# The first two column groups of the per-layer gate as a pair: seven products for eight in three of eight units, with the weights' sums made by VectorE

## The chip, the cores and the metric

The kernel runs on one core of a Trainium2 chip. The metric is the device time of one launch in microseconds (us); the median of three runs counts. PE is TensorE, DVE VectorE, ACT ScalarE, POOL GpSimd and SP SyncE, which here issues DMAs.

## The reference

One layer of a decoder trunk with 256 tokens, width 2048, all in f32. Only the end of it is touched:

```
h = RMSNorm(x);  u = h @ W_in          # ten parts; two of them the merge gates ga, gb
...                                    # two branches: yA (short conv), yB (linear recurrence)
m = sigmoid(gA) * (yA @ WA) + sigmoid(gB) * (yB @ WB);  x = x + m @ W_o
gate = sigmoid(RMSNorm(x) @ W_pg)      # W_pg 2048 x 2048: "the last gate"
x = x + gate * (p @ W_pp);  out = RMSNorm(x)
```

## The kernel before

**Products.** Each f32 operand is cut into two parts of 32-bit type fp32r: hi, a rounded copy (ACT), and lo, what is left (DVE subtracts). A product is a `triple` of matmuls: hi·hi, hi·lo, lo·hi, each 128 x 128 of the activations (loaded as PE's weights) against 512 columns of the weight matrix, summed in a PSUM bank. `put` cuts activations, 256 columns at a time; `cut`, called from `split`, cuts weights.

**Items.** The work is one flat list of items. An item is a chunk `c` of 256 rows of a weight matrix and a column group of 512 columns (`whi`, `wlo`, 128 x 1024: the two halves of 128 rows beside each other); with two halves of tokens that makes four products or 12 matmuls. The groups come in order: PP, the ten parts of W_in, A, B, then O (W_o, four groups of eight items, the first two interlaced) and PG (the last gate, four groups of eight items). The last PG group is not in the loop, but in a tail that orders its halves for the end. In what follows, G is the first item of the last gate (`gate` in the code), G−1 the last item of O's group 3, and so on; O3 is that group, and O2 the one before it, whose last item is G−9.

**The order.** In the loop over `pos`, an item first causes the `split` of the items up to `pos + LEAD` (3 ahead; from `gate` on growing to 8, function `ahead`). Then its matmuls are traced, then loads of raw weights (`load`, SP; three buffers of 1 MB), then `advance()` makes one step of every running epilogue. Epilogues are generators; each `yield` ends a step. A first step is traced at the group's last item, behind that item's `advance()`. A split needs a free pair (whi, wlo): a ring of four in `wp`, and from G+4 on six more in the pool `late`, so that the pair of an item is that of the item four before.

What is traced is put in order by the framework's scheduler, which can move an instruction past others of its engine. `step` makes an epilogue's ACT and DVE work follow the newest split. `pinned(mark)`, called at the end of an item, goes further: it ties each instruction that ACT and DVE got in this item to the one traced before it on that engine, so that traced order is kept; its first tie is to the last instruction of the item before. Before the change this is done from the first pair of merge gates to the end of the last B group, not in O and PG.

**An O epilogue** (`ep_o`, five steps). Step one: DVE adds the two banks to x (L840), ACT squares for the norm (L841) and copies in spread order (L847), SP writes 4 x 128 KB to DRAM (`turn`, L317). Step two: SP issues the reload of 512 KB (L328). Two steps only wait. Step five: a DVE transpose (L321) and four `put`s (L286 ACT, L287 DVE), which make four of the sixteen 128-row pieces of `x1T`, the activations of the last gate. O2's fifth step is traced at G−5, and O3's at G+3.

**A PG epilogue** (`ep_pg`): ACT sigmoid from PSUM, DVE times `pw` and added to x, ACT squares, a step later POOL times the final gain.

**Merge gates as pairs.** Two column groups of W_in (ga, gb) are worked on together for j = 1 to 3: five of the eight chunks are units "S" of Winograd's form, with seven products in place of eight, the others are "C" items with four products for each of the two groups. The seven sums go to eight banks, four of tag `g` and four of tag `s`; `ep_products` and `ep_gates` add them up. A unit needs sums of the tokens' quarters (s1 to s4) and of the weights' quarters (t1 to t4). For these pairs DMAs on POOL's queue add part of the weights (`add_by_dma`), and `combine_weights` does the rest.

Of the kernel before, what the change touches and what calls it, by code (L numbers as in the profile page):

```python
# [15 lines left out]
P = 128  # L16
# [15 lines left out]
SEVEN = [()] + 3 * [(0, 2, 3, 5, 6)]  # L32
TOGETHER = [(0, 1), (1, 2), (3, 2)]
NARROW, Q = len(LEVELS), 32

# [12 lines left out]
def hybrid_kernel(ctx, tc, xT, x, pT, prm, gfin, masks, w_in, w_a, w_b, w_o, w_pg, w_pp, out):  # L48
# [58 lines left out]
    for gi, (kind, j, w, g, op) in enumerate(groups):  # L107
        if kind == "gb" and SEVEN[j]:
            continue
        for c in range(w.shape[2]):  # L110
            it = {"gi": gi, "kind": kind, "j": j, "c": c, "last": c == w.shape[2] - 1}
            if kind != "ga" or not SEVEN[j]:
                key = ("PP", j // 2) if kind == "PP" else (gi, c // 2)
                items.append(dict(it, w=(w, g, c), raw=key, slot=(j if kind == "PP" else c) % 2))
            elif c in SEVEN[j]:
                items.append(dict(it, kind="S", w=(w, g, c), raw=(gi, c)))
# [10 lines left out]
    def raw_of(pos):  # L127
        it = items[pos]
        if it["raw"] not in loaded:
            if it["kind"] == "S":  # L130
                t = tuple(
                    pools["st"].tile([P, n, CW], F32, tag=tag, bufs=bufs, name=nm(tag))
                    for tag, n, bufs in (("sA", 2, 2), ("sB", 1, 3))
                )
            else:
                t = wp.tile([P, 2, 2 * CW], F32, tag="raw", bufs=3, name=nm("raw"))
            loaded[it["raw"]] = t
        return loaded[it["raw"]]

    def load(pos):  # L140
        it = items[pos]
        if it["raw"] not in loaded:
            raw, (w, g, c) = raw_of(pos), it["w"]
            if it["kind"] == "S":
                for n, to in enumerate(raw):
                    nc.sync.dma_start(out=to.rearrange("p n x -> p (n x)"), in_=w[g + n, :, c, n * CW :])
            elif it["kind"] == "C":
                for n in range(2):
                    nc.sync.dma_start(out=raw[:, n, :], in_=w[g + n, :, c, :])
            elif pos < APART:  # L150
                for i in range(2):
                    w, g, c = items[pos + i]["w"]
                    nc.sync.dma_start(out=raw[:, i, :], in_=w[g, :, c, :])
            else:
                nc.sync.dma_start(out=raw, in_=w[g, :, c : c + 2, :])

    def add_by_dma(behind=None):
        pos = next((n for n, it in enumerate(items) if it["kind"] == "S" and n not in pair_sums), None)
        if pos is not None:
# [18 lines left out]
    def pair_of(pool, n, tags=("whi", "wlo"), width=2 * CW):  # L178
        return tuple(pool.tile([P, width], F32R, tag=tag, bufs=n, name=nm(tag)) for tag in tags)

    def cut(hi, lo, src):
        a = nc.scalar.activation(out=hi, in_=src, func=AF.Copy)  # L182
        v = nc.vector.tensor_tensor(out=lo, in0=src, in1=hi.bitcast(F32), op=ALU.subtract)  # L183
        state["splits"] = (a.ins, v.ins)

    def split(pos, halves=(0, 1)):
        it = items[pos]
        load(pos)
        src = raw_of(pos)
        src = src[0].rearrange("p n x -> p (n x)") if it["kind"] == "S" else src[:, it["slot"], :]  # L190
# [21 lines left out]
    last_group = len(items) - w_pg.shape[2]  # L212
    gate = len(items) - 4 * w_pg.shape[2]
    parked = next(n for n, it in enumerate(items) if it["kind"] == "A" and it["j"] == 3)
# [500 lines left out]

    def quarters(j):
        return [state[n][:, t * CW : (t + 1) * CW] for n in ("ga", "gb") for t in range(NT)]

    def ep_products(j, bk):
        for n in ("ga", "gb"):  # L720
            state[n] = t4(n, 1)
        a0, a1, b0, b1 = quarters(j)
# [6 lines left out]
    def ep_gates(j, n, bk):  # L729
        q = quarters(j)  # L730
        for t in range(NT):
            add(q[2 * n + t], q[2 * n + t], bk["c", n, t])
        for t in range(NT):
            d = q[2 * n + t]
            nc.scalar.activation(out=d, in_=d, func=AF.Sigmoid, scale=state["rstd1"][:, t : t + 1])
# [9 lines left out]
    def ep_gb(j, psum):  # L745
        return ep_gate(j, "gb", psum)

    def token_sums():
# [5 lines left out]
        for first, n in TOGETHER:  # L754
# [12 lines left out]
            a11, a12, a21, a22 = Fv[:, :, 0, 0], Fv[:, :, 1, 0], Fv[:, :, 0, 1], Fv[:, :, 1, 1]  # L767
            s1, s2, s3, s4 = (Sv[:, :, i] for i in range(4))
            for out, u, v, op in (
                (s1, a21, a22, ALU.subtract), (s2, s1, a11, ALU.subtract),  # L770
                (s3, a11, a21, ALU.subtract), (s4, a12, s2, ALU.add),
            ):
                nc.vector.tensor_tensor(out=out, in0=u, in1=v, op=op)
            sums_of = tuple(v[:, first : first + n] for v in state["S"])
            fourth = tuple(v[:, 2 * c : 2 * (c + n) : 2, P:] for v in state["hT"])
            for (hi, lo), src in ((sums_of, Sv[:, :, :3]), (fourth, Sv[:, :, 3])):
                nc.scalar.activation(out=hi, in_=src, func=AF.Copy)
                nc.vector.tensor_tensor(out=lo, in0=src, in1=hi.bitcast(F32), op=ALU.subtract)
# [56 lines left out]
    def ep_o(j, psum):  # L835
# [15 lines left out]
        for c in range(4):  # L851
            put(state["x1T"], j * 4 + c, x1[:, c * T : (c + 1) * T], gain(PRM_GPLE, j * 4 + c))
        if j == 3:
            tot = sc(2, "tot2", 1)
# [3 lines left out]
            )  # L858
            state["rstd2"] = rsqrt_of(tot, NT, D, "r2")

    def ep_pp(j, psum):
# [191 lines left out]
    def ahead(pos):  # L1053

        return LEAD + min(max(pos - gate, 0) // 4, 5)

# [10 lines left out]

    def count_products(j):
        order = [it for it in items if it["kind"] in ("S", "C") and it["j"] == j]
        used.clear()  # L1070
# [15 lines left out]
    def unit_products(pos):  # L1086
        it = items[pos]
        c, h = it["c"], state["hT"]

# [10 lines left out]
        b22, t1, t3, t2, t4_ = sums.pop(pos)  # L1100
        s1, s2, s3 = (tuple(v[:, SEVEN[1].index(c), i] for v in state["S"]) for i in range(3))
        s4 = x_of(0, 1)
        for name, op, part in zip(names, (s4, x_of(0, 0), x_of(1, 0), s1, s3, s2, x_of(1, 1)),
# [20 lines left out]
    for pos, it in enumerate(items[:last_group]):  # L1124
        mark = len(nc.cur_bb.bb.instructions)
        kind, j, c, last = (it[n] for n in ("kind", "j", "c", "last"))
        _, _, w, g, opname = groups[it["gi"]]
        nch = w.shape[2]
        if pos == gate:
            close_pool("back")  # L1130
            close_pool("m")
            open_pool("late", "left")
        if pos == parked:
# [4 lines left out]
            active.append(unpark())  # L1138
        if pos + 2 < len(items) and items[pos + 2]["kind"] == "S":
# [22 lines left out]
        if pos >= gate and c == 0:  # L1162
            load_pw(j)
        if pos == FIRST + 4:
# [13 lines left out]
        if kind in ("S", "C"):  # L1178
            if c == 0 and it.get("n", 0) == 0:
                count_products(j)  # L1180
                for name, tag in zip(("P6", ("c", 0, 1), "P5", "P7", "P1", ("c", 0, 0), ("c", 1, 0), ("c", 1, 1)), "ggggssss"):
                    banks[name] = bank(tag)
            if kind == "C" and c == nch - 1 and it["n"] == 0:
                ep_products(j, banks)
            unit_products(pos)
            if kind == "C" and c == nch - 1:
                ep_gates(j, it["n"], banks)
        else:
# [9 lines left out]

        for q in range(done, min(done + AHEAD, len(items)) if pos >= FIRST else 0):
            load(q)  # L1200
# [17 lines left out]
        if last and kind not in ("S", "C"):  # L1218
# [110 lines left out]
```

## Time and profile before

| | |
|---|---|
| median of three runs | 815.23 us (814.61 to 815.31) |
| the profiled execution's own time | 816.18 us |
| its span, first to last instruction | 813.3 us |
| mean granted clock of TensorE | 0.996 |
| O group 3 on PE | 694.9 to 716.7 us of the span |
| last gate on PE, groups 0 and 1 | 716.7 to 760.2 us |

A row of a timeline gives the start, the length, the engine, the line of the kernel, the operation with out<-in, a count, and in brackets the idle time before it and what ended that. A row of groups gives the count, the busy time, the mean in ns, and the idle time ahead of the group's instructions by what ended it. A row of a table by stretches gives the busy time of each engine with the number of its instructions, then the granted clock, the share of the DMA engines that is busy, and GB/s. Of a merged row the length runs from the first start to the last end.

### The profile page before, as it was taken

To read this page: it belongs to the slowest core of one execution; us is meant where nothing else is said; L and a number is where in the kernel's file an instruction comes from. 1 tells how busy PE (TensorE), PEld (TensorE's weight loads), DVE (VectorE), ACT (ScalarE), POOL (GpSimd) and SP (SyncE) were. 2 spreads that over 40 slices of the span, in tenths; PEclk is the share of its full clock that TensorE was granted. 3 is DMA by queue.
4 is the path that set the end of the run, shared out by engine and by line. 5 is a ranking of instruction groups with operands and counts; after the bars stand their busy time and mean duration, and the time that the engine had idled before them with its cause. 6 is when DMAs were issued, how large, how long until landed. Compare 5 with 4: busy or idle time off the path is not lost.

```text
span 813.3 us, 10660 instructions
## 1 busy us (share of the span) xinstructions
PE 803.0 (99%) x4059; PEld 664.8 (82%) x4059; DVE 589.0 (72%) x748; ACT 458.3 (56%) x617; POOL 49.4 (6%) x58
## 2 busy tenths in 40 slices
PE   9999999999999999999999999999999999999995
PEld 6888888888888888888888888888888888888885
DVE  6746588767776498767679988987988665677932
ACT  7576476465555466466456456456544456566623
POOL 1000000001000000000021210210000000000310
PEclk9999999999999999999999999999999999999998
DMA  9988565648867555647799996995844779887812
GB/s 337 389 309 290 196 206 168 235 134 274 253 236 255 184 184 201 207 157 262 269 328 295 317 312 209 318 313 203 255 160 173 277 255 323 302 268 255 309 43 103
DMA packets 52659, 198.52 MB, mean 244 GB/s; under 512 B 6784, under 2 KB 16256, under 8 KB 37888
## 3 DMA queue, kind: packets, MB, share of 16 engines
q1 hardware_dynamic: 43200, 174.78, 61.2%
q0 software_dynamic: 6384, 16.25, 8.4%
q10 hardware_dynamic: 3024, 6.82, 2.5%
q8 instruction: 31, 0.51, 0.2%
q14 instruction: 20, 0.16, 0.1%
HBM read 184.19 MB, written 13.63 MB: 243 GB/s over the span
## 4 chain that ended last, share of the span: by engine, by line
PE 96%; issue 1%; DMA 1%; ACT 0%; DVE 0%; POOLq 0%; POOL 0%
PE g L1059 29%; PE g L1061 29%; PE g L1060 29%; PE s L1060 3%; PE s L1061 3%; PE s L1059 3%; DMA raw<-in_w_pp 1%; PE s L497 1%; PE s L598 0%; PE s L617 0%; PE s L616 0%; PE s L615 0%; ACT xs L922 0%; DVE wlo L183 0%; PE s L589 0%
## 5 line engine op out<-in xcount | busy, mean ns | idle before, releaser
L183 DVE TENSOR_TENSOR wlo<-raw,whi 128x1024 fp32r<-128x1024 f32 (+1 forms) x264 | 319.8, 1227 | 160.9 <-ACT whi L182 159.0
L182 ACT ACTIVATE whi<-raw 128x1024 fp32r<-128x1024 f32 (+1 forms) x264 | 272.2, 1049 | 207.4 <-PE g L1061 172.6
L1059 PE MATMUL g<-whi,xh 128*128 128x512 f32 (+1 forms) x738 | 284.0, 385 | 0.0
L1060 PE MATMUL g<-wlo,xh 128*128 128x512 f32 (+1 forms) x738 | 283.9, 385 | 0.0
L1061 PE MATMUL g<-whi,xl 128*128 128x512 f32 (+1 forms) x738 | 283.7, 385 | 0.0
L1061 PEld LDWEIGHTS g<-whi,xl 128*128 128x128 f32 x738 | 138.7, 188 | 27.6
L1059 PEld LDWEIGHTS g<-whi,xh 128*128 128x128 f32 x738 | 138.7, 188 | 27.4
L1060 PEld LDWEIGHTS g<-wlo,xh 128*128 128x128 f32 x738 | 138.7, 188 | 27.3
L1060 PE MATMUL g<-wlo,mh 128*128 128x512 f32 x128 | 49.8, 389 | 0.0
L1061 PE MATMUL g<-whi,ml 128*128 128x512 f32 x128 | 49.8, 390 | 0.0
L1059 PE MATMUL g<-whi,mh 128*128 128x512 f32 x128 | 49.7, 389 | 0.0
L182 ACT ACTIVATE thi<-sA 128x1024 fp32r<-128x1024 f32 x15 | 15.9, 1062 | 32.6 <-DVE sA L714 20.3
L1060 PE MATMUL s<-wlo,xh 128*128 128x512 f32 x84 | 32.7, 389 | 0.0
L1059 PE MATMUL s<-whi,xh 128*128 128x512 f32 x84 | 32.7, 389 | 0.0
L1061 PE MATMUL s<-whi,xl 128*128 128x512 f32 x84 | 32.7, 389 | 0.0
L1061 PEld LDWEIGHTS g<-whi,ml 128*128 128x128 f32 x128 | 23.9, 188 | 5.2 <-DVE ml L791 0.3
L1059 PEld LDWEIGHTS g<-whi,mh 128*128 128x128 f32 x128 | 24.0, 188 | 5.0
L1060 PEld LDWEIGHTS g<-wlo,mh 128*128 128x128 f32 x128 | 24.0, 188 | 5.0
L1060 PE MATMUL g<-wlo,ybTh 128*128 128x512 f32 x64 | 24.9, 390 | 0.0
L1061 PE MATMUL g<-whi,ybTl 128*128 128x512 f32 x64 | 24.9, 390 | 0.0
L1060 PE MATMUL g<-wlo,yaTh 128*128 128x512 f32 x64 | 24.9, 389 | 0.0
L1061 PE MATMUL g<-whi,yaTl 128*128 128x512 f32 x64 | 24.9, 389 | 0.0
(218 smaller groups left out, 906.5 us busy)
## 6 DMA issues: line engine op xcount, KB each, us to landing
raw<-in_w_in SPq DMA_DIRECT2D x66, 1024.0 KB, 5.1
raw<-in_w_o SPq DMA_DIRECT2D x16, 1024.0 KB, 6.1
raw<-in_w_pg SPq DMA_DIRECT2D x16, 1024.0 KB, 6.6
sT<-in_w_in POOLq DMA_DIRECT2D x30, 512.0 KB, 9.6
raw<-in_w_in SPq DMA_DIRECT2D x28, 512.0 KB, 5.8
raw<-in_w_a SPq DMA_DIRECT2D x8, 1024.0 KB, 8.8
raw<-in_w_b SPq DMA_DIRECT2D x8, 1024.0 KB, 8.6
sA<-in_w_in SPq DMA_DIRECT2D x15, 512.0 KB, 7.7
```

What stands on the lines that cost most here:

```text
L182: a = nc.scalar.activation(out=hi, in_=src, func=AF.Copy)
L183: v = nc.vector.tensor_tensor(out=lo, in0=src, in1=hi.bitcast(F32), op=ALU.subtract)
L497: nc.tensor.matmul(out, X[:, 0, h, s], X[:, 1, h, t], start=True, stop=True, tile_position=(0, i * n))
L1059: nc.tensor.matmul(psum, oh, hi, start=first, stop=False)
L1060: nc.tensor.matmul(psum, oh, lo, start=False, stop=False)
L1061: nc.tensor.matmul(psum, ol, hi, start=False, stop=last)
```

## The change

PG's groups 0 and 1 become one pair. Chunks 2, 4 and 6 are units (`LATE_SEVEN`), with 21 matmuls each; chunks 0, 1, 3, 5 and 7 are two C items each. So 16 items with 192 matmuls become 13 items (10 C, 3 S) with 183, in the order G (chunk 0, group 0), G+1 (chunk 0, group 1), G+2, G+3 (chunk 1), G+4 (unit, chunk 2), G+5, G+6, G+7 (unit, chunk 4), G+8, G+9, G+10 (unit, chunk 6, `settled`), G+11, G+12. Group 2 begins at G+13.

- Both column groups of a chunk lie in one raw tile, loaded by two DMAs of 512 KB. `split` cuts the first group's weights as before. `combine_late`, an item after the split, cuts b22 (512 columns), adds four times 512 columns in the raw tile on DVE, and cuts the tile's two halves of 1024, which now hold the sums.
- `late_sums` makes the tokens' sums of a unit: an add of 512 columns, four of 128, a cut of 512. Its steps come behind the epilogue of the O group with the unit's rows: O1 for chunk 2, O2 for chunk 4, O3 for chunk 6.
- Pairs of buffers come from `free_pair`, which takes the one of `wp` or `late` that is free first. The lead is 3 at the beginning of the gate and 4 up to `settled`, then grows as before; loads look one item less far ahead.
- `ep_products` and `ep_gates` add up the pair's banks at its last two items; `ep_pg` of both groups follows there. `load_pw(1)` is called at G+1.
- The pool `back` is closed at O2's first item instead of G.
- `pinned` is also called from G−4 to G+13.

```diff
+LATE_SEVEN = (2, 4, 6)
...
-        if kind == "gb" and SEVEN[j]:
+        if kind == "gb" and SEVEN[j] or (kind, j) == ("PG", 1):
             continue
+        units = {"ga": SEVEN[j % len(SEVEN)], "PG": LATE_SEVEN if j == 0 else ()}.get(kind, ())
...
+    rings = {"wp": 4 * [-1], "late": 6 * [-1]}
+
+    def free_pair(until):
+        names = [n for n in rings if n == "wp" or n in pools]
+        name = min(names, key=lambda n: rings[n][0])
+        rings[name] = rings[name][1:] + [until if until < last_group else len(items)]
+        return pair_of(pools.get(name, wp), len(rings[name]))
...
         if pos not in parts:
-            spare = pos >= gate and (pos - gate) % 10 >= 4
-            parts[pos] = pair_of(pools["late"], 6) if spare else pair_of(wp, 4)
+            parts[pos] = free_pair(pos)
...
+    def combine_late(pos):
+        R = raw_of(pos)
+        (b11, b21), (b12, b22) = ([R[:, n, i * CW : (i + 1) * CW] for i in range(2)] for n in range(2))
+        hi, lo = pair_of(pools["late"], 1, ("bhi", "blo"), CW)
+        cut(hi, lo, b22)
+        ts = [(hi, lo)]
+        add(b11, b11, b12)
+        add(b12, b12, b22)
+        add(b22, b11, b22)
+        add(b21, b22, b21)
+        for n in range(2):
+            hi, lo = free_pair(pos)
+            cut(hi, lo, R[:, n, :])
+            ts += [(hi[:, i * CW : (i + 1) * CW], lo[:, i * CW : (i + 1) * CW]) for i in range(2)]
+        b22, t1, t4_, t3, t2 = ts
+        sums[pos] = (b22, t1, t3, t2, t4_)
...
+        for c in LATE_SEVEN:
+            if c // 2 == j:
+                yield
+                yield from late_sums(c)
...
+    def late_sums(c):
...
+        f = t4()
+        F, Sv = f[:, :CW].rearrange("p (r b t) -> p r b t", r=2, b=2), f[:, CW:].rearrange("p (s t) -> p s t", s=4)
+        hi, lo = (v[:, 2 * c : 2 * c + 2, :] for v in state["x1T"])
+        add(F.rearrange("p r b t -> p r (b t)"), hi.bitcast(F32), lo.bitcast(F32))
+        yield
+        sums_of(F[:, 0, 0], F[:, 1, 0], F[:, 0, 1], F[:, 1, 1], [Sv[:, i] for i in range(4)])
+        cut(*(v[:, LATE_SEVEN.index(c)] for v in state["late sums"]), Sv)
+        yield
...
-        return LEAD + min(max(pos - gate, 0) // 4, 5)
+        return LEAD + min(max(pos - gate, 0) // 4, 5 if pos >= settled else 1)
...
+        for q in range(pos + 1, done):
+            if items[q]["kind"] == "S" and items[q]["op"] != "hT" and q not in sums:
+                combine_late(q)
...
+                if it["op"] != "hT":
+                    order = ("P1", "P6", "P5", "P7", c00, c01, c10, c11)
...
-        for q in range(done, min(done + AHEAD, len(items)) if pos >= FIRST else 0):
+        for q in range(done, min(done + AHEAD - (gate - LEAD <= pos < settled), len(items)) if pos >= FIRST else 0):
             load(q)
...
-        if begun < pos < parked + 8:
+        if begun < pos < parked + 8 or gate - 4 <= pos < settled + 4:
             pinned(mark)
```

More of the change, by code (lines that the diff above doesn't have):

```diff
@@ L157, in add_by_dma @@
     def add_by_dma(behind=None):
-        pos = next((n for n, it in enumerate(items) if it["kind"] == "S" and n not in pair_sums), None)
+        pos = next((n for n, it in enumerate(items) if it["kind"] == "S" and it["op"] == "hT" and n not in pair_sums), None)
         if pos is not None:
@@ L212, in hybrid_kernel @@
     last_group = len(items) - w_pg.shape[2]
-    gate = len(items) - 4 * w_pg.shape[2]
+    gate = next(n for n, it in enumerate(items) if it["op"] == "x1T")
+    settled = max(n for n, it in enumerate(items) if it["kind"] == "S")
     parked = next(n for n, it in enumerate(items) if it["kind"] == "A" and it["j"] == 3)
@@ L746, in ep_gb, with sums_of @@
         return ep_gate(j, "gb", psum)
+    def sums_of(a11, a12, a21, a22, to):
+        s1, s2, s3, s4 = to
+        for out, u, v, op in (
+            (s1, a21, a22, ALU.subtract), (s2, s1, a11, ALU.subtract),
+            (s3, a11, a21, ALU.subtract), (s4, a12, s2, ALU.add),
+        ):
+            nc.vector.tensor_tensor(out=out, in0=u, in1=v, op=op)
     def token_sums():
@@ L859, in ep_o @@
             state["rstd2"] = rsqrt_of(tot, NT, D, "r2")
+    def late_sums(c):
+        if "late sums" not in state:
+            n = len(LATE_SEVEN)
+            both = pair_of(pools["tmp3"], 1, ("shi", "slo"), n * 4 * P)
+            state["late sums"] = tuple(v.rearrange("p (u s t) -> p u s t", u=n, s=4) for v in both)
+        f = t4()
[6 more added lines that the diff above has]
+        yield
     def ep_pp(j, psum):
@@ L1066, in hybrid_kernel, with count_products @@
     used, left = {}, {}
-    def count_products(j):
-        order = [it for it in items if it["kind"] in ("S", "C") and it["j"] == j]
+    def count_products(gi):
+        order = [it for it in items if it["kind"] in ("S", "C") and it["gi"] == gi]
         used.clear()
@@ L1087, in unit_products @@
         it = items[pos]
[L1088 removed]
+        c, h = it["c"], state[it["op"]]
         def x_of(r, t):
@@ L1128, in hybrid_kernel @@
         nch = w.shape[2]
+        if kind == "O" and j == 2 and c == 0:
+            close_pool("back")
         if pos == gate:
-            close_pool("back")
             close_pool("m")
```

66 lines of the change are left out of this document (36 added, 30 removed).

## The prediction

> **What bounds the kernel now.** I read the page first (busy shares, then the chain), then PE's timeline around the start of the last gate, then a table by stretches, then the DVE, ACT and SP timelines of the same microseconds.
>
> ```profile
> PE 803.0 (99%) x4059; PEld 664.8 (82%) x4059; DVE 589.0 (72%) x748; ACT 458.3 (56%) x617; POOL 49.4 (6%) x58
> PE 96%; issue 1%; DMA 1%; ACT 0%; DVE 0%; POOLq 0%; POOL 0%
> 711.69 0.39 PE L1061 MATMUL g<-whi,ml 128*128 128x512 f32 x1
> 716.45 0.39 PE L1061 MATMUL g<-whi,ml 128*128 128x512 f32 x1
> 716.67 0.39 PE L1059 MATMUL g<-whi,xh 128*128 128x512 f32 x1
> 721.89 0.39 PE L1061 MATMUL g<-whi,xl 128*128 128x512 f32 x1
> core 0: us, PE busy (x) PEld busy (x) DVE busy (x) ACT busy (x) POOL busy (x), PEclk, DMA share, GB/s
> 694.90:716.70 21.80, 21.80 (x98) 18.04 (x97) 12.88 (x14) 11.25 (x15) 0.00 (x0) 1.00 0.86 289
> 716.70:738.40 21.70, 21.70 (x97) 18.00 (x96) 16.50 (x22) 14.78 (x24) 0.72 (x1) 1.00 0.84 294
> 738.40:760.20 21.80, 21.80 (x98) 18.02 (x97) 16.95 (x17) 13.07 (x18) 4.06 (x2) 1.00 0.73 250
> ```
>
> PE ends the span and never waits around the change: in the three stretches PE is busy for the whole length. The matmuls overlap, so their 0.39 us is latency; what counts is the step. From 711.69 to 721.89 there are 45 steps: 0.2267 us each. An item (12 matmuls) takes 2.72 us. The last gate (item G) starts at 716.67, so G−1 starts at 713.95, and two groups of it last 16 × 2.72 = 43.5 us, to 760.2. DVE has slack now: (16.50 + 16.95) / 43.5 = 77% busy in them.
>
> **What goes.** A unit has seven products for eight, three matmuls each. Three units drop 9 matmuls of 192: 9 × 0.2267 = **2.04 us**, all on the path. That is the whole possible gain; nothing else shortens PE's stream, since PE waits for nothing here that could disappear.
>
> **What is added, and on which engine.** Durations:
>
> ```profile
> L183 DVE TENSOR_TENSOR wlo<-raw,whi 128x1024 fp32r<-128x1024 f32 x260 | 317.1, 1236 | 160.0 <-ACT whi L182 158.1
> L182 ACT ACTIVATE whi<-raw 128x1024 fp32r<-128x1024 f32 x260 | 269.7, 1055 | 206.5 <-PE g L1061 172.6 <-DMA raw<-in_w_pg 12.5 <-issue 10.9
> L714 DVE TENSOR_TENSOR sA<-sA 128x512 f32<-128x512 f32 x15 | 10.4, 692 | 0.5
> L183 DVE TENSOR_TENSOR blo<-sB,bhi 128x512 fp32r<-128x512 f32 x15 | 10.2, 683 | 0.0
> L182 ACT ACTIVATE bhi<-sB 128x512 fp32r<-128x512 f32 x15 | 9.3, 620 | 7.7 <-PE s L1061 7.7
> L773 DVE TENSOR_TENSOR tlo<-thi 128x128 f32<-128x128 f32 x2 | 0.6, 282 | 0.0
> ```
>
> Before, a chunk of a column pair costs DVE two subtractions of 1024 (2.47 us). A unit costs three (3.71), one of 512 (0.68) and four adds of 512 (2.77), and for the token sums an add (0.69), four of 128 (1.13) and a subtraction of 512 (0.68): 9.66 us for 4.76 us of PE. Extra on DVE: 3 × 7.19 = 21.6 us; on ACT 3 × (1.06 + 2 × 0.62) = 6.9. Of DVE's, 16.6 falls into the pair (the token sums of two units, 2.5 each, are traced ahead of G), where 10 us were idle: DVE becomes the bound there, and its order counts.
>
> **What moves: the order.** The change pins DVE and ACT to traced order from G−4 on, each first new instruction behind the last one traced before. Traced last before G−4 is the fifth step of O2's epilogue: a transpose that waits for a reload from DRAM, then four `put`s (ACT, DVE). So the weight split of G−1 comes behind them on both engines. Now it does not:
>
> ```profile
> 705.99 1.06 ACT L182 ACTIVATE whi<-raw 128x1024 fp32r<-128x1024 f32 x1 [1.66 <-PE g L1061]
> 715.25 1.23 DVE L183 TENSOR_TENSOR wlo<-raw,whi 128x1024 fp32r<-128x1024 f32 x1 [1.49 <-ACT whi L182]
> 716.39 1.24 DVE L321 STREAM_TRANSPOSE t<-t 128x1024 f32<-128x1024 f32 x1
> 717.55 1.25 DVE L840 TENSOR_TENSOR xs<-xs,g 128x512 f32<-128x512 f32 x2
> 701.38 2.17 SPq L317 DMA_DIRECT2D turn<-t  x4
> 708.46 0.34 SPq L328 DMA_DIRECT2D t<-turn  x1
> DMA to landing us min/median/max: 6.3/6.3/6.3
> 692.85 1.71 ACT L286 ACTIVATE xh<-t,prm_t 128x256 fp32r<-128x256 f32 x4 [1.50 <-DVE t L321]
> L287 DVE SCALAR_TENSOR_TENSOR xl<-t,prm_t,xh 128x256 fp32r<-128x256 f32 x32 | 13.6, 476 | 0.6 <-ACT xh L286 0.6
> ```
>
> G−1 is split at 705.99, the moment G−5 ends (716.67 − 4 × 2.72 = 705.79); the transpose runs at 716.39, behind the split of G+2, though it is traced before that of G−1. That traced order does hold up a split in the pinned stretch can be seen in the B group, where ACT idles for a transpose and only then cuts weights:
>
> ```profile
> 617.55 1.06 ACT L790 ACTIVATE mh<-back 128x1024 fp32r<-128x1024 f32 x1 [2.82 <-DVE back L321]
> 618.52 1.04 ACT L182 ACTIVATE whi<-raw 128x1024 fp32r<-128x1024 f32 x1
> ```
>
> Worked on the clock of before, each engine strictly in order (back to back a 1024 subtraction starts 1.14 after the one before, as 715.25 and 716.39 show, ACT's cut about 1.0; an add of 512 0.69):
>
> *Stall at G−1.* The reload (708.46) lands 6.3 later, at 714.8. Transpose to 716.1, ACT's four halves of the puts to 717.8 (0.40 apart), cut of G−1 to 718.8, its subtraction 718.85 to 720.1. PE wanted both at 713.95 and 714.2: it waits 4.9 and then 1.0, **6.0 us**. G starts at 722.6.
>
> *Stall at G+3.* O3's first step, by its rows:
>
> ```profile
> L840 DVE TENSOR_TENSOR xs<-xs,g 128x512 f32<-128x512 f32 x8 | 5.1, 676 | 0.0
> L841 ACT ACTIVATE t<-xs 128x512 f32<-128x512 f32 x8 | 4.9, 614 | 0.0
> L847 ACT ACTIVATE t<-xs 128x512 f32<-128x512 f32 x8 | 4.6, 621 | 0.1
> ```
>
> DVE, after G−1, does G, G+1, G+2 and the second unit's token sums (2.6 with the wait for ACT's cut), and is free at 726.6, 3.8 after O3's last product. O3's two adds, squares and copies end at 729.7 on ACT, which then cuts G+3; its subtraction ends at 732.0. PE wants it at 731.1: **1.0 us** with 0.06 at G+1.
>
> *First unit, G+4.* Subtraction of G+4 731.9, the 512 one 733.0, four adds to 736.2, ACT cuts the first sums by 737.25, DVE subtracts by 738.5 and the second by 739.7. PE reaches the unit at 734.5, has nine matmuls without the sums (to 736.6), and waits 0.74 + 1.04 + 0.46 = **2.2 us**.
>
> *Second unit, G+7.* In its way stand G+5, G+6 (to 741.9), O3's transpose and puts, G+7, G+8, the third unit's token sums. The reload:
>
> ```profile
> 722.78 1.75 SPq L317 DMA_DIRECT2D turn<-t  x4
> 729.20 0.34 SPq L328 DMA_DIRECT2D t<-turn  x1
> DMA to landing us min/median/max: 4.8/4.8/4.8
> ```
>
> From first write to reload 6.4 here, 7.1 at O2: 6.75; landing 4.8 and 6.3: 5.55. Copies end at 729.7, so the reload lands at 742.1. Transpose and puts to 745.7, G+7 and G+8 to 748.5, token sums (with ACT's cut between) to 751.4, the 512 cut 752.0, adds 754.5, sums cut and subtracted 756.8 and 758.0. PE is there at 747.0 and needs the first product's low part, then the sums: 4.32 + 0.58 + 1.72 + 1.04 + 0.46 = **8.1 us**. That reload is no cause of it: with it in at once DVE is late by its work alone, and the sum is 7.7. Third unit: DVE has 8 us more of PE's time by then, wait 0.
>
> Hidden, at nothing: the pair's end (one ACT copy, eight DVE operations of about 0.69, 5.5 us) beside the two last items and five items of lead; without that cover PE would wait for the banks of group 2, at most 5.5 us. Eight more issues on SP (512 KB instead of 1024), 0.34 each (the reload's row, also 512 KB), on a queue that mostly waits for a buffer:
>
> ```profile
> SPq L155 <- DVE wlo L183: 81.1, 19, 8.0
> ```
>
> If that slack were gone, ACT would wait for a landing. `load_pw(1)` is seven items earlier, with its buffer free. Banks: the first C items use the `s` banks, so O's `g` banks are not waited for.
>
> Sum: 6.0 + 1.0 + 2.2 + 8.1 = 17.3 of waits less 2.04: **+15.3 us**. On the profiled execution (span 813.3, its time 816.18) 831.5; its time is 0.95 above the median, so 815.23 + 15.3 = **830.5**.
>
> Bounds: the first stall goes from 0 (the reload in by 708.8) to 7.7 (O1's token sums, traced ahead of O2's epilogue, delay it by 1.7); the last from 0 (if DVE had kept another order) to 8.9.
>
> One rule weighs against the first stall. The Trainium skill, "DMA: Bandwidth & Descriptors" (section on the anatomy of one DMA), gives, as a fit for DMAs issued from GpSimd, about 2.0 us plus the bytes over 436 GB/s; as an estimate by that page 3.2 us for this reload and 2.3 for a write. By it the reload would be in by 710, before G−1 starts, and the sum would be that of the rival B. The rows (6.3 and 4.8 here) disagree, so I stay with them.
>
> **The rivals.** *A', the clock falls too.*
>
> ```profile
> 804.23 0.28 PE L1061 MATMUL g<-whi,xl 128*128 128x256 f32 x1
> 806.00:810.00 4.00, 0.00 (x0) 0.00 (x0) 1.30 (x3) 1.81 (x4) 0.55 (x1) 0.59 0.34 125
> 1.46 3.43 PE L951 MATMUL s<-warm 128*128 128x512 bf16 x8 [1.46 <-DVE warm L947]
> ```
>
> After PE's last matmul (804.5) the granted clock falls: 0.59 over 806 to 810 means half speed from about 806.7. The first eight matmuls of the run took 3.43 us, not 8 × 0.2267 = 1.81. A wait of 4.9 and one of 4.3 could each cost 1.6: 832 to 834. The Trainium skill, "TensorE: Matmul & The Clock Gate" (part 1), states this as halving after an idle window of some 3.4 us; the end of this trace agrees, but no wait of this length lies inside the run.
>
> *B, only DVE's work binds*: the transposed block of O2 does not stand before G−1 (the reload is early, or the pin reaches less far back). G then starts in time with DVE caught up; the first unit is just in time, and the second still waits 7.7 to 8.0. Net +5.6 to +6.0: 821.
>
> *C, faster*: DVE's order leaves the sums in time. Place: the second unit; price: no waits, −2.04, so 813.2. It decides at whether DVE has the second unit's last sums by G + 23.8 (G+7 starts at 21.1, twelve matmuls on): it needs 3.0 for O3's first step, six subtractions (6.8), two units of adds and cuts (13.5 with ACT's turn), transpose and puts 3.5, token sums 2.9: about 30. Only if O3's epilogue ran behind the second unit would it hold. Against it stands the pin, for it that an unpinned order did defer such a block by four splits (716.39). *D*: waits of 0.4 to 3.7 eat about the gain.
>
> **How the numbers follow.** A 0.47 (830.5), A' 0.15 (832 to 834), B 0.17 (821), C 0.16 (813.2), D 0.05 (815). The range takes A, A', B and D: 815.0 to 835.0; out of it are C and 0.03 above. A measurement tells about 0.2% (1.6 us): faster 0.16 (C), same 0.05 (D), slower 0.79 (A, A', B).
>
> **What would show it.** A holds if, after the change, DVE's transpose of O2's block runs before the subtraction of G−1, and PE has about 6 us of idle just before G, waiting for ACT's and DVE's parts of the weights; if PE waits again at the first and longest at the second unit, for the subtractions of the sums; and if nothing is waited for at the third, nor in group 2. A transpose that still runs behind several splits makes it B; a PE row without waits makes it C; a granted clock under 1.00 in these stretches makes it A'. I am wrong altogether if the traced order is not what the engines run.

## The result and the profile after

| | before | after |
|---|---|---|
| median | 815.38 us (814.61 to 816.06, 6 runs) | 837.57 us (836.52 to 838.52, 6 runs) |
| the profiled execution | 816.18 us | 837.98 us |
| its span | 813.3 us | 836.2 us |
| mean granted clock of TensorE | 0.996 | 0.986 |

The ratio is 1.0271, 95% interval 1.0258 to 1.0284: slower, by 22.2 us. The line numbers of after are other ones: the matmuls are L1113, L1114 and L1115, ACT's cut of weights is L192, DVE's subtraction L193, the transpose L351, the puts L316 (ACT) and L317 (DVE), the weights' adds L744, the sigmoid of the last gate L935.

The page of the profile after, busy shares and the chain by engine:

```profile
PE 811.4 (97%) x4050; PEld 666.5 (80%) x4050; DVE 612.4 (73%) x792; ACT 465.1 (56%) x627; POOL 47.3 (6%) x58
PE 84%; DVE 6%; DMA 4%; ACT 3%; issue 2%; SPq 0%; POOLq 0%; POOL 0%; ACTq 0%; DVEq 0%
```

PE has its nine matmuls less, and DVE about 23 us more work, but a share of 73% in place of 72%. The chain, which was 96% PE, now passes through DVE, DMA and ACT for 13% of the span. What PE waits for (us in total, times, longest):

```profile
PE g L1113 <- ACT whi L192: 11.1, 6, 3.8
PE g L1114 <- DVE wlo L193: 1.6, 3, 0.8
PE s L1113 <- ACT bhi L192: 1.4, 1, 1.4
PE s L1114 <- DVE blo L193: 0.3, 1, 0.3
PE g L1113 <- ACT t L753: 0.2, 1, 0.2
```

PE nearly always waits for ACT's cut of weights. PE's timeline gives the places:

```profile
717.13 1.22 PE L1113 MATMUL g<-whi,mh 128*128 128x512 f32 x2 [2.62 <-ACT whi L192]
...
736.04 0.50 PE L1113 MATMUL g<-whi,shi 128*128 128x512 f32 x1 [0.96 <-ACT whi L192]
...
749.79 0.49 PE L1113 MATMUL s<-bhi,shi 128*128 128x512 f32 x1 [1.38 <-ACT bhi L192]
...
754.46 0.79 PE L1113 MATMUL g<-whi,shi 128*128 128x512 f32 x1 [3.07 <-ACT whi L192]
...
785.20 0.73 PE L1113 MATMUL g<-whi,xh 128*128 128x512 f32 x2 [0.40 <-ACT whi L192]
786.70 0.50 PE L1114 MATMUL g<-wlo,xh 128*128 128x512 f32 x1 [0.76 <-DVE wlo L193]
...
795.78 1.22 PE L1113 MATMUL g<-whi,xh 128*128 128x512 f32 x2 [3.80 <-ACT whi L192]
797.44 0.80 PE L1114 MATMUL g<-wlo,xh 128*128 128x512 f32 x1 [0.44 <-DVE wlo L193]
```

From top to bottom: item G−1 (its activations are still `mh`), the first unit G+4 (`shi` are the tokens' sums), the second unit G+7 twice, and then, ahead of group 2's last items, G+17 and G+19, two places that the prediction did not have. A bracket tells less than the loss, since matmuls overlap: I take each step from start to start less 0.2267 us a matmul, and sum by place. G−1 loses 4.7 us, G to G+3 0.25, the first unit 1.8, G+6 and the second unit 0.7 + 7.35 = 8.0, the third unit nothing, the change to group 2 0.5, and group 2 1.7 + 7.6 = 9.3. That is 24.5; the span's growth of 22.9 and the 2.04 that went make 24.9.

Part of each of the three largest losses is the clock. A table by stretches of the changed kernel:

```profile
core 0: us, PE busy (x) PEld busy (x) DVE busy (x) ACT busy (x) POOL busy (x), PEclk, DMA share, GB/s
717.20:721.00 3.80, 3.76 (x9) 2.56 (x10) 3.77 (x7) 0.83 (x1) 0.00 (x0) 0.58 0.43 115
718.33:754.44 36.11, 29.77 (x119) 22.34 (x118) 27.92 (x41) 17.19 (x26) 0.00 (x0) 0.93 0.60 204
745.00:765.00 20.00, 14.86 (x54) 10.64 (x54) 16.75 (x26) 8.25 (x11) 1.63 (x1) 0.83 0.31 114
754.40:758.50 4.10, 4.04 (x10) 3.01 (x11) 4.03 (x6) 3.37 (x5) 0.21 (x1) 0.57 0.18 23
795.70:802.50 6.80, 6.28 (x14) 4.50 (x15) 6.16 (x5) 3.82 (x5) 0.60 (x1) 0.51 0.60 209
```

Behind the three longest waits PE works at about half speed: 3.76 × 0.42 + 4.04 × 0.43 + 6.28 × 0.49 = 1.6 + 1.7 + 3.1 = 6.4 us of the 24.5, an estimate from the first row and the last two. The row from 745 to 765 says what DVE is doing around the second unit: it is idle for 3.25 of 20 us, while PE is idle for 5.1. And from the end of G−1's subtraction (718.33) to the first subtraction of the second unit's sums (754.44) it was idle for 8.2 of 36.1 us, about what PE lost at that unit. So DVE's work alone does not explain the wait; DVE stands in a line. Experiment 1 bears this out: without the pin PE does not wait at the second unit.

The first line is that of G−1, on DVE and ACT:

```profile
713.15 1.25 DVE L351 STREAM_TRANSPOSE t<-t 128x1024 f32<-128x1024 f32 x1 [7.16 <-DMA t<-turn]
714.43 1.70 ACT L316 ACTIVATE xh<-t,prm_t 128x256 fp32r<-128x256 f32 x4 [9.70 <-DVE t L351]
714.97 1.68 DVE L317 SCALAR_TENSOR_TENSOR xl<-t,prm_t,xh 128x256 fp32r<-128x256 f32 x4 [0.58 <-ACT xh L316]
717.11 1.22 DVE L193 TENSOR_TENSOR wlo<-raw,whi 128x1024 fp32r<-128x1024 f32 x1 [0.46 <-ACT whi L192]
```

DVE is idle for 7.16 us and ACT for 9.70, until O2's reload lands; then come transpose and puts, and only at 717.11 the subtraction of G−1. Before, ACT cut this item at 705.99, and the transpose ran behind the split of G+2. This is the prediction's picture, line by line.

The last line, ahead of group 2's end, is the one it lacked:

```profile
777.87 0.73 ACT L935 ACTIVATE t<-t,r2r 128x512 f32<-128x512 f32 x1 [4.29 <-DVE t L744]
778.63 0.69 DVE L938 TENSOR_TENSOR t<-t,pw 128x512 f32<-128x512 f32 x1 [0.26 <-ACT t L935]
780.08 0.63 ACT L940 ACTIVATE t<-xs 128x512 f32<-128x512 f32 x1 [1.48 <-DVE xs L939]
780.71 0.71 ACT L935 ACTIVATE t<-t,r2r 128x512 f32<-128x512 f32 x1
781.45 1.27 DVE L938 TENSOR_TENSOR t<-t,pw 128x512 f32<-128x512 f32 x1 [1.40 <-ACT t L935]
...
784.11 1.99 ACT L192 ACTIVATE whi<-raw 128x1024 fp32r<-128x1024 f32 x2
785.18 2.60 DVE L193 TENSOR_TENSOR wlo<-raw,whi 128x1024 fp32r<-128x1024 f32 x2 [1.74 <-ACT whi L192]
788.41 0.73 ACT L935 ACTIVATE t<-t,r2r 128x512 f32<-128x512 f32 x1 [2.31 <-DVE t L744]
...
794.69 4.83 ACT L192 ACTIVATE whi<-raw 128x1024 fp32r<-128x1024 f32 x5
795.76 5.03 DVE L193 TENSOR_TENSOR wlo<-raw,whi 128x1024 fp32r<-128x1024 f32 x4 [0.60 <-ACT whi L192]
```

`ep_pg` of the pair's two groups is traced inside the pinned stretch, token half by token half: sigmoid on ACT, a product and an add on DVE, square on ACT, and again. In traced order the two engines take turns: from the adds that feed the first sigmoid, about 777, to 784 for one group and 787.7 to 794.8 for the other. DVE is idle for a quarter to a third of these two stretches and ACT for half or more. The splits of G+17 and G+18 are traced behind the first epilogue (ACT cuts them from 784.11 on) and those of G+19 and G+20 behind the second (from 794.69 on).

### The profile page after: what moved, and what is told of

Its sections match the earlier page's. It is cut to its first block, busy times and chain, and to the rows that moved or that the text cites. A ratio compares the mean times of both kernels' runs of the same rounds, so it can differ in the third digit from the quotient of the medians.

```text
span 836.2 us, 10704 instructions
## 1 busy us (share of the span) xinstructions
PE 811.4 (97%) x4050; PEld 666.5 (80%) x4050; DVE 612.4 (73%) x792; ACT 465.1 (56%) x627; POOL 47.3 (6%) x58
## 4 chain that ended last, share of the span: by engine, by line
PE 84%; DVE 6%; DMA 4%; ACT 3%; issue 2%; SPq 0%; POOLq 0%; POOL 0%; ACTq 0%; DVEq 0%
PE g L1114 24%; PE g L1113 24%; PE g L1115 24%; PE s L1115 3%; PE s L1114 3%; PE s L1113 3%; DVE wlo L193 2%; DMA raw<-in_w_pg 2%; DMA t<-turn 2%; ACT whi L192 1%; DVE raw L744 1%; PE s L527 1%; DMA turn<-t 1%; DVE t L938 0%; DVE t L351 0%
## 5 line engine op out<-in xcount | busy, mean ns | idle before, releaser
L193 DVE TENSOR_TENSOR wlo<-raw,whi 128x1024 fp32r<-128x1024 f32 (+1 forms) x267 | 319.8, 1216 | 155.8 <-ACT whi L192 154.1
L192 ACT ACTIVATE whi<-raw 128x1024 fp32r<-128x1024 f32 (+1 forms) x267 | 274.1, 1048 | 202.4 <-PE g L1115 162.5
L1113 PE MATMUL g<-whi,xh 128*128 128x512 f32 (+1 forms) x677 | 261.6, 387 | 4.4 <-ACT whi L192 4.2
L1114 PE MATMUL g<-wlo,xh 128*128 128x512 f32 (+1 forms) x677 | 261.4, 386 | 1.6 <-DVE wlo L193 1.6
L1115 PE MATMUL g<-whi,xl 128*128 128x512 f32 (+1 forms) x677 | 260.8, 386 | 0.0
L1113 PEld LDWEIGHTS g<-whi,xh 128*128 128x128 f32 x677 | 127.7, 189 | 30.8 <-ACT whi L192 5.0
L1114 PEld LDWEIGHTS g<-wlo,xh 128*128 128x128 f32 x677 | 127.9, 189 | 28.2 <-DVE wlo L193 3.1
L1115 PEld LDWEIGHTS g<-whi,xl 128*128 128x128 f32 x677 | 127.8, 189 | 25.4
L1113 PE MATMUL g<-whi,mh 128*128 128x512 f32 x128 | 50.0, 395 | 2.6 <-ACT whi L192 2.6
L1114 PE MATMUL s<-wlo,xh 128*128 128x512 f32 x130 | 50.9, 392 | 0.0
L1115 PE MATMUL s<-whi,xl 128*128 128x512 f32 x130 | 50.7, 390 | 0.0
L1113 PE MATMUL s<-whi,xh 128*128 128x512 f32 x130 | 50.7, 391 | 0.0
L1114 PE MATMUL g<-wlo,mh 128*128 128x512 f32 x128 | 50.5, 394 | 0.0
L1115 PE MATMUL g<-whi,ml 128*128 128x512 f32 x128 | 50.2, 394 | 0.0
L192 ACT ACTIVATE thi<-sA 128x1024 fp32r<-128x1024 f32 x15 | 15.9, 1062 | 32.5 <-DVE sA L744 20.3
L1113 PEld LDWEIGHTS g<-whi,mh 128*128 128x128 f32 x128 | 24.3, 191 | 8.1 <-ACT whi L192 3.0
L1114 PEld LDWEIGHTS s<-wlo,xh 128*128 128x128 f32 x130 | 24.5, 189 | 5.6 <-DVE wlo L193 0.3
L1114 PEld LDWEIGHTS g<-wlo,mh 128*128 128x128 f32 x128 | 24.3, 190 | 5.8 <-DVE wlo L193 0.8
L1113 PEld LDWEIGHTS s<-whi,xh 128*128 128x128 f32 x130 | 24.7, 190 | 5.0
L1115 PEld LDWEIGHTS s<-whi,xl 128*128 128x128 f32 x130 | 24.5, 189 | 5.1
L1115 PEld LDWEIGHTS g<-whi,ml 128*128 128x128 f32 x128 | 24.2, 190 | 5.3 <-DVE ml L827 0.3
L1115 PE MATMUL g<-whi,ybTl 128*128 128x512 f32 x64 | 24.9, 389 | 0.0
```

Source lines behind the costliest of these rows:

```text
L1113: nc.tensor.matmul(psum, oh, hi, start=first, stop=False)
L1114: nc.tensor.matmul(psum, oh, lo, start=False, stop=False)
L1115: nc.tensor.matmul(psum, ol, hi, start=False, stop=last)
```

## The experiments

**Theories.** *The pin*: what costs the time is the strict order from G−4 to G+13, which puts instructions that wait (for a reload, for O3's block, for the other engine) ahead of splits that could run. *The work*: DVE's 21.6 us more are the cost, and an order only moves it. If the pin, then without it the kernel is near before; if the work, then nearly nothing changes without it. In what follows "the changed kernel" is 837.57 us, 1.0271; before, in the same comparisons, was 815.0 to 815.1.

**1. Without the pin at the gate.**

```diff
-        if begun < pos < parked + 8 or gate - 4 <= pos < settled + 4:
+        if begun < pos < parked + 8:
```

> The change with its new pin taken out (order of ACT and DVE from G-4 to G+13 left to the scheduler); the pair, its units and their sums stay. Theory O (the pinned order makes the waits): O2's transpose runs behind splits again, so the wait at G-1 (2.8 + 0.8, with the half clock after it 4.7 us) goes, and the waits in group 2 (9.5 us with the clock) shrink to under 2; the units may still wait. 837.6 - 4.7 - 8 = 825 or less. Theory W (VectorE has simply too much to do in the pair, in any order): the time stays above 833.

Measured: 816.07 us, 1.0014 (1.0004 to 1.0023). The pin costs 21 us (1.0271 less 1.0014, times 815). That decides between the theories, and by more than expected. What is left of the work shows in the stretches of this kernel:

```profile
716.70:738.40 21.70, 21.16 (x94) 17.10 (x93) 20.69 (x31) 13.99 (x22) 0.00 (x0) 1.00 0.67 222
738.40:760.20 21.80, 20.31 (x89) 16.27 (x88) 21.70 (x32) 12.80 (x18) 2.89 (x1) 1.00 0.57 208
```

Now DVE (the third busy time of a row) is busy for 42.4 of 43.5 us, so here its work is the bound; experiment 8 tests this. PE loses 2.8 us by its steps, 0.8 at the first unit and 2.0 at the third, against the 2.04 that nine matmuls give.

**2. The pin from G instead of G−4.**

```diff
-        if begun < pos < parked + 8 or gate - 4 <= pos < settled + 4:
+        if begun < pos < parked + 8 or gate <= pos < settled + 4:
```

> The change with its pin beginning at G instead of G-4; its end and all else as in the change. The first tie is then to O3's first step, and O2's transpose is free. Theory O (the first tie puts O2's reload ahead of the split of G-1): the wait of 2.8 + 0.8 with its half clock goes, the other waits stay: 837.6 - 4.7 = 833; the first unit's wait may change by a microsecond, since DVE comes to it caught up. Rival: the wait comes back at the first unit, as in the run with the longer lag: 836.

Measured: 833.31 us, 1.0218 (1.0203 to 1.0234). The wait at G−1 is gone, those at the units and in group 2 are about as in the changed kernel. The first tie costs 4.3 us (0.0053 × 815); the place's 4.7 in the profile agrees.

**3. The pin up to the third unit only.**

```diff
-        if begun < pos < parked + 8 or gate - 4 <= pos < settled + 4:
+        if begun < pos < parked + 8 or gate - 4 <= pos <= settled:
```

> The change with the pin from G-4 to G+10 only, so that the pair's last two items and G+13 are free in order. Theory E (in traced order the two PG epilogues are ping-pong between ACT and DVE, 6.4 us each, with the splits of G+17 to G+20 behind them): the waits in group 2 (1.7 + 5.2, 9.5 with the half clock) go, the ones at G-1 and at the units stay: 837.6 - 9.5 = 828. Rival: the pair's end waits because its ten products of banks and adds take DVE's time, in any order: over 834.

Measured: 829.27 us, 1.0178 (1.0161 to 1.0195). The waits of this kernel:

```profile
PE g L1113 <- ACT whi L192: 7.0, 4, 3.1
```

11.1 in six waits became 7.0 in four: the two of group 2 are gone. The last three items of the pin cost 7.6 us (0.0093 × 815). They hold the pair's sums and both epilogues, and this run does not tell these apart; experiment 4 changes the epilogues alone.

**4. The pin kept, both sigmoids ahead of DVE's products.**

```diff
         for t in range(NT):
-            s = slice(t * CW, (t + 1) * CW)
-            d = xs[:, t, j * CW : (j + 1) * CW]
             nc.scalar.activation(
-                out=gt[:, s], in_=psum[t], func=AF.Sigmoid, scale=state["rstd2"][:, t : t + 1]
+                out=gt[:, t * CW : (t + 1) * CW], in_=psum[t], func=AF.Sigmoid, scale=state["rstd2"][:, t : t + 1]
             )
+        for t in range(NT):
+            s = slice(t * CW, (t + 1) * CW)
+            d = xs[:, t, j * CW : (j + 1) * CW]
             nc.vector.tensor_tensor(out=gt[:, s], in0=gt[:, s], in1=pw[:, s], op=ALU.mult)
```

> The change with its pin, but in the PG epilogue both sigmoids are traced ahead of DVE's products, so that ACT and DVE change over twice less for a group. Theory E (ping-pong in traced order is what group 2 waits for): each of the two epilogues gets about 2 us shorter, and the wait of 3.96 + 1.21 with its half clock goes to about 1: 837.6 - 6 = 832. Rival (the splits wait for PE's last products of the pair, whatever the order within the epilogue): 837.

Measured: 832.80 us, 1.0217 (1.0203 to 1.0231). The order inside the epilogues is worth 4.4 us as long as it is strict. Of group 2's waits, 1.09 stays at the head, in place of 3.80:

```profile
791.17 0.73 PE L1114 MATMUL g<-whi,xh 128*128 128x512 f32 x2 [1.09 <-ACT whi L192]
```

**5. The pin alone, on the kernel before.** All of its work and its items are those of before; only the ties are added, over the same items.

```diff
-        if begun < pos < parked + 8:
+        if begun < pos < parked + 8 or gate - 4 <= pos < gate + 14:
```

> The kernel before, with no pair at all, and only the pin added, from G-4 over 18 items of the last gate (into its second group). Theory O: the pin by itself costs the wait at G-1, 4.7 us with the half clock behind it, plus what O3's block makes late: the split of G+7 then stands behind a transpose whose reload lands some 18 us after G, which is about when it is wanted, so 0 to 4 more; the PG epilogue of group 0 is traced over in ping-pong once, 6.4 us on two engines, with a lead of 4 items (11 us) that covers it: 820 to 825. Rival: the pin only hurts together with the pair's extra work: 815 to 816.

Measured: 820.09 us, 1.0061 (1.0046 to 1.0076): slower by 5.0 us with not one operation added. In its profile PE waits at one place in the gate, G−1:

```profile
PE g L1059 <- ACT whi L182: 2.2, 1, 2.2
PE g L1060 <- DVE wlo L183: 0.5, 1, 0.5
```

By steps that is 3.25 us, and the granted clock stays at 1.00 there. The profiled execution, 818.39 us, was the shortest of four; the others took 819.66 to 822.10 at a mean granted clock of 0.994 or 0.995, in place of 0.997. Where these lost more is in no profile; falls of the clock would fit, but that is not shown. So the first stall belongs to the pin alone; the stalls at the units and in group 2, which this profile does not have, need the pin and the pair's work together.

**6. O2's and O3's transposes traced later.** O2's is then traced at G−1 and O3's at G+5 (an item that is a unit makes two steps of the epilogues), so the pin is kept, but the block stands behind other splits.

```diff
-        x1 = yield from turned(x1, 3)
+        x1 = yield from turned(x1, {2: 7, 3: 6}.get(j, 3))
```

> The change with a longer lag between reload and transpose, 7 steps for O2 and 6 for O3 (3 before), pin kept. O2's transpose is then traced behind the split of G+2, and O3's behind the second unit's sums. Theory O: no wait at G-1 (-4.7 us), and at the second unit the 8.0 us shrink by what the transpose, its puts and the token sums take of DVE (7) to about 1: 837.6 - 4.7 - 7 = 826. Group 2 waits as before. Theory W: the second unit waits as long as before, 833.

Measured: 835.36 us, 1.0246 (1.0231 to 1.0261). A miss: only 2 us came of it. The wait at G−1 is gone, but others grew. O2's block, four items later, now delays the first unit (a wait of 3.13 us there), and O3's stands ahead of the third unit's cuts:

```profile
750.46 1.24 DVE L351 STREAM_TRANSPOSE t<-t 128x1024 f32<-128x1024 f32 x1
...
756.77 2.86 DVE L744 TENSOR_TENSOR raw<-raw 128x512 f32<-128x512 f32 x4
759.67 1.06 ACT L192 ACTIVATE whi<-raw 128x1024 fp32r<-128x1024 f32 x1 [4.75 <-DVE raw L744]
760.78 0.71 PE L1113 MATMUL s<-whi,xh 128*128 128x512 f32 x1 [3.61 <-ACT whi L192]
```

The transpose starts at once, since its data is there; DVE's adds for the third unit come at 756.77, ACT waits 4.75 us for them, and PE 3.61. In a strict order the block (transpose 1.25, puts 1.7, tokens' sums some 2.5 us on DVE) has to stand somewhere, and in the places tried somebody stood behind it. That no place would do is not shown.

**7. The edits of 6, 3 and 4 together.**

```diff
-        x1 = yield from turned(x1, 3)
+        x1 = yield from turned(x1, {2: 7, 3: 6}.get(j, 3))
...
-        if begun < pos < parked + 8 or gate - 4 <= pos < settled + 4:
+        if begun < pos < parked + 8 or gate - 4 <= pos <= settled:
...
```

> Both of the two runs above at once, and in the PG epilogue both sigmoids traced ahead of DVE's products. Theory O with E: what the single runs gain adds up, 837.6 - 11.7 - 9.5 = 816.4, the first unit's 1.6 us and the pair's end left: 815 to 818, about the time of before or a little under or over. Theory W: not under 825.

Measured: 827.55 us, 1.0153 (1.0138 to 1.0168). A miss for the same reason: group 2 is clean, but the waits at the first unit (3.1 and 0.2) and around the third (3.9 and 1.0) are about those of experiment 6. No hand-made order tried here comes near the scheduler's own (816.07).

**8. Without the pin, without the four adds.**

```diff
-        add(b11, b11, b12)
-        add(b12, b12, b22)
-        add(b22, b11, b22)
-        add(b21, b22, b21)
...
```

The other line of this diff is the pin's, as in experiment 1. What is left out are the weights' sums, so this kernel computes something else and serves only to show their price.

> The change without its pin and without the four adds of each unit (what is left out: the weights' sums, so that the units multiply unsummed quarters; cuts, token sums and matmuls stay). It shows what the nine matmuls are worth when VectorE has room: 12 adds of 0.69, 8.3 us of DVE, are gone from the pair, where DVE was busy 42.4 of 43.5 us without the pin. If the units' 2.8 us of waits are DVE's work, they go: 815.1 - 2.0 = 813.1. If they are something else (the loads, the pairs of buffers), they stay: 816.

Measured: 813.12 us, 0.9974 (0.9965 to 0.9984). PE waits for nothing in the last gate, and the nine matmuls give what they should: 815.13 less 813.12 is 2.0, the sum was 2.04. So 2.9 us of the 816.07 are these 12 adds (8.3 us of DVE).

**9 to 11. Without the pin, other units.** One unit, two, and three in a row; the other line of the diff is the pin's, as in experiment 1.

```diff
-LATE_SEVEN = (2, 4, 6)
+LATE_SEVEN = (4,)
```

> No pin, one unit (chunk 4): three matmuls saved, 0.68 us, and no waits: 815.1 - 0.7 = 814.4. If the pair itself costs anything beside its units (two loads of 512 KB for one, the banks' sums, two PG epilogues on one another), it shows here as 815 or more.

Measured: 814.38 us, 0.9990 (0.9982 to 0.9999), as expected. So the pair itself, with its loads in two parts, its buffers and its two epilogues at the end, costs nothing that shows without the pin.

```diff
-LATE_SEVEN = (2, 4, 6)
+LATE_SEVEN = (3, 5)
```

> No pin, and two units (chunks 3 and 5) in place of three (2, 4, 6): six matmuls fewer than before, 1.36 us; 9.7 us less DVE work in the pair, no token sums behind O3's epilogue, the first unit two items later. Theory W' (without the pin only DVE's work is left, and it is the third unit that is too much): no waits, 815.1 - 1.4 = 813.8, faster than both kernels. Rival: the first unit waits for its sums as it did (0.8) and the loads of the pair's end cost too: 815.

Measured: 813.55 us, 0.9983 (0.9974 to 0.9992). This version beats both kernels, if only by 0.2% against before. Its stretches:

```profile
716.70:738.40 21.70, 21.70 (x97) 17.97 (x96) 19.51 (x30) 14.31 (x22) 1.09 (x1) 1.00 0.82 281
738.40:760.20 21.80, 21.80 (x98) 18.06 (x97) 21.59 (x28) 13.36 (x17) 0.00 (x0) 1.00 0.66 240
```

PE is busy for the whole length again, DVE for 41.1 of 43.5 us. Six matmuls are 1.36 us, and the medians differ by 1.6.

```diff
-LATE_SEVEN = (2, 4, 6)
+LATE_SEVEN = (3, 4, 5)
```

> No pin, three units, chunks 3, 4 and 5 in place of 2, 4 and 6: nine matmuls saved, 2.04 us. No unit depends on O3's tokens, the first comes two items later, but three stand in a row. Theory W' (DVE's work is the limit: 9.7 us a unit against 4.8 of PE): DVE falls behind by 4.9 a unit in a row, with a lead of four items (10.9 us), so the third waits: 1 to 3 us, 814 to 816. Rival (O3's epilogue was the trouble): no waits, 813.1.

Measured: 821.11 us, 1.0075 (1.0062 to 1.0087), worse than expected. The same work as in experiment 1, but without C items between the units:

```profile
PE g L1113 <- ACT whi L192: 3.7, 5, 1.2
```

Each unit has 9.7 us of DVE work, 7.2 without the tokens' sums, for 4.76 us of PE, and the lead of four items does not bridge three of them. By steps PE loses 8.0 us, with a stretch at half clock among them (last section).

**12. Experiment 10's version, with the sigmoids first.** Units 3 and 5, no pin, and `ep_pg` as in experiment 4.

```diff
-LATE_SEVEN = (2, 4, 6)
+LATE_SEVEN = (3, 5)
```

> No pin, units 3 and 5, and both sigmoids of a PG epilogue ahead of DVE's products. PE has no wait left in the run with units 3 and 5, so nothing is left to gain there but the shape of the end: 813.5, as that run; a gain over 0.5 us would mean that PE's waits are not all there is.

Measured: 813.66 us, 0.9983 (0.9974 to 0.9992): no difference. An order that cost 4.4 us under the pin costs nothing where the scheduler may move instructions.

## Why the prediction was right or wrong

The sign held, and so did the cause, the strict order of the pin (experiment 1); the time did not. 837.57 lies 7 us above the forecast and 2.6 above the range.

- **The gain**, −2.04: right. Experiment 8 shows 2.0 where no wait is in the way.
- **G−1**, 6.0: right in its mechanism, and experiments 2 and 5 show it alone. 4.7 by steps, of which 1.6 is the clock, so the wait itself is 3.1, half of the forecast. The reload, issued at 708.32, was there at 713.15, after 4.8 us; I had taken the 6.3 that it took before; the 4.8 of O3's reload, quoted a little further down, was the better guide.
- **G+3**, 1.0: it was 0.25. With G−1 later by less, less was late behind it.
- **First unit**, 2.2: 1.8. **Second unit**, 8.1: 8.0 with G+6, but that this agrees is partly luck: the 8.1 were all waiting, the 8.0 are 6.3 of waiting and 1.7 of clock. **Third unit**, 0: right.
- **The step that failed** is "Hidden, at nothing: the pair's end (one ACT copy, eight DVE operations of about 0.69, 5.5 us) beside the two last items and five items of lead". I counted `ep_products` and the adds of `ep_gates`, and the banks that they free (0.5 us, so that was nearly hidden). I did not count that `ep_gates` traces `ep_pg` of both groups inside the pin, where ACT and DVE take turns for about 6.4 us a group with the splits of G+17 to G+20 behind them. From 773.10 to 784.11 ACT cut no weights at all: 4.29 us of that it waited for the pair's sums on DVE, and 6.3 it was in the first epilogue. The place cost 9.3 us in the profile, of which 3.1 is the clock; experiment 3 takes it away and experiment 4 halves it. That is more than the distance from forecast to result.
- **A'**, the clock: I gave it as a rival, with 1.6 us for each long wait. The first two cost 1.6 and 1.7, and it belonged into the sum: waits of 4.9 and 4.3 us were forecast, and in the rows of before the clock had fallen 2.2 us after PE's last matmul (804.5 to 806.7), so that falls followed from the rows at hand. Those 2.2 us are less than the 3.4 us of idling that I took them to agree with; the last section shows what they do agree with. The fall in group 2 took 3.1.
- **The rivals B and C** rested on the order being looser than the pin's. It was strict. But experiment 1 shows what C's argument said for it: without the pin the scheduler defers such blocks, and the kernel is within 0.14% of before. That DVE's own work would still cost 7.7 in strict order, as B has it, has not been tried by itself: no run has the pin only between the two places that experiments 2 and 3 free. What is left for that middle, 21 less 4.3 less 7.6, is about 9 us, if the parts add up.

The expectations for experiments 6 and 7 erred in the same manner as the failed step: I moved a block and asked only who had stood behind it, not who would.

## What to carry to other kernels

A strict order across two engines turns each wait of one instruction into a wait of everything traced behind it; before pinning a stretch, list all that is traced in it, the epilogues of its last items too, and for each entry what it waits for and which split is next. An engine that idles for a part of the time in which PE waits for it is a sign of order, as DVE here, idle for 8.2 of 36.1 us; one that is busy nearly throughout, 42.4 of 43.5 us in experiment 1, is a sign of work. Here the first was worth 21 us and the second 2.9. Where an engine gets several times its share of work in units, spread the units and take only as many as its slack holds: two gave 1.6 us, three took 1.0.

## What the runs showed of the hardware

The granted clock halves inside the run and comes back, and it does so on a grid. In the changed kernel it is 0.50 from 717.00 to 720.41, from 751.13 to 757.96 and from 795.50 to 802.33 us, and 1.00 between these. The steps from one change to the next are 3.41, 30.72, 6.83, 37.54 and 6.83 us, all whole multiples of 3.41 (1, 9, 2, 11 and 2 times). Cut into stretches of that grid, the changed kernel reads:

```profile
713.58:717.00 3.42, 0.93 (x5) 0.43 (x3) 2.49 (x5) 2.57 (x6) 0.00 (x0) 1.00 0.00 0
717.00:720.41 3.41, 3.24 (x7) 2.14 (x8) 3.27 (x5) 1.03 (x2) 0.00 (x0) 0.50 0.30 62
734.06:737.48 3.42, 2.24 (x9) 1.26 (x8) 2.26 (x4) 2.55 (x3) 0.00 (x0) 1.00 0.88 317
747.72:751.13 3.41, 1.71 (x6) 0.69 (x5) 2.68 (x7) 1.15 (x2) 0.00 (x0) 1.00 0.01 2
751.13:754.54 3.41, 0.34 (x2) 0.08 (x1) 2.19 (x5) 1.19 (x2) 0.00 (x0) 0.50 0.00 0
792.09:795.50 3.41, 0.00 (x0) 0.00 (x0) 3.04 (x3) 2.50 (x4) 1.30 (x2) 1.00 0.11 23
```

The stretches ahead of the three falls have PE busy for 0.93, 1.71 and 0.00 of 3.41 us. The one at the first unit (734.06), with a wait of 0.96 us and one of 0.22, has it busy for 2.24, and no fall follows. The second fall shows that it is not the length of one wait that counts: it comes at 751.13, 3.3 us before the wait of 3.07 ends, so what led to it are the waits of 1.38 and 0.31 us in the stretch before; that of 3.07 only kept the clock down.

In the other profiles, too, all changes of the clock lie whole multiples of 3.41 us apart, and the same border holds. Experiment 5's two stretches around G−1, then the second of those in experiment 4, then the stretch ahead of the fall in experiment 11 and the one behind it:

```profile
711.88:715.29 3.41, 2.05 (x10) 1.36 (x8) 2.59 (x5) 1.89 (x5) 0.00 (x0) 1.00 0.00 0
715.29:718.71 3.42, 2.08 (x8) 1.42 (x9) 2.96 (x4) 3.42 (x4) 0.00 (x0) 1.00 0.25 36
```

```profile
715.27:718.68 3.41, 1.83 (x7) 1.24 (x8) 2.95 (x5) 1.95 (x3) 0.00 (x0) 1.00 0.13 12
```

```profile
742.74:746.16 3.42, 1.63 (x6) 0.73 (x5) 3.42 (x8) 3.42 (x7) 0.00 (x0) 1.00 0.61 248
746.16:749.57 3.41, 3.41 (x8) 2.18 (x8) 3.38 (x5) 0.65 (x1) 0.00 (x0) 0.50 0.00 0
```

In experiments 4 and 5 the wait at G−1, 2.2 us and a shorter one, lies across a border of the grid, so neither stretch has much of it, and the clock stays. In experiment 11 waits of at most 1.2 us lie close together in one stretch, and it falls. Over all profiles every stretch at full clock with PE busy for 1.71 us or less (0.50) was followed by a fall, and none with 1.83 or more (0.54); busy times of PE are modelled, so the border is only as good as these. A fall lasts one stretch or two in the waits here: one when PE was busy again for nearly all of the first (3.24 us at 717.00), two when it was not (0.34 at 751.13).

The Trainium skill, "TensorE: Matmul & The Clock Gate" (part 1, the HAM clock gate), ties the fall to an idle window of about 3.4 us that runs free of the program. The traces agree, with 3.41 us; and a stretch had the effect of an idle one here already when PE was busy for half of it. Where the borders lie differs from execution to execution (717.00 in the changed kernel, 715.29 in experiment 5), so the same wait can cost a fall in one and none in another. That the clock would have held with other matmuls put into the waits was not tried.
